# Both projections of a hybrid mLSTM and SSD layer as one level of seven-product block multiplication

## The chip, the cores and the metric

One NeuronCore of a Trainium2 chip runs the whole layer in one launch. The metric is device time in microseconds. PE is TensorE, PEld its weight loads, DVE VectorE, ACT ScalarE, POOL GpSimd; SP is SyncE, which issues nearly all transfers.

## The reference

The layer takes 2048 tokens of 1024 channels in float32:

```python
h = rms_norm(x, norm_w)
proj = h @ w_in                                  # 1024 x 6680
q, k, v, i_pre, f_pre, o_pre, z_m, z_s, xbc, dt_raw = jnp.split(proj, SPLIT_POINTS, axis=-1)
hm = mlstm_chunkwise(q, k, v, log_i, log_f)      # 4 heads, chunks of 128 tokens
hm = head_norm(hm) * mlstm_norm_w * sigmoid(o_pre) * silu(z_m)
xs, Bm, Cm = split(silu(causal_depthwise_conv(xbc, conv_w, conv_b)))
y = ssd_chunked(xs, dt, A, Bm, Cm) + d_skip * xs # 16 heads in 2 groups, chunks of 128 tokens
y = group_norm(y * silu(z_s)) * ssd_norm_w
x = x + concat([hm, y]) @ w_out                  # 2048 x 1024
return rms_norm(x, final_norm_w)
```

## The kernel before

The 2048 tokens are taken in four segments of 512. `prep_seg` normalises a segment and transposes it, so that channels lie on partitions. Every operand of a projection is held as two tiles, a rounded part (`hi`, an ACT copy, L140, L210, L711) and the rest (`lo`, a DVE subtraction, L141, L212, L712), and a product is three matmuls: hi by hi, hi by lo, lo by hi. `load_block` loads and splits a block of `w_in` columns, again for every segment. `ch_group` (L222 to L224) gives channels on partitions for 512 tokens, `tk_group` (L234 to L236) tokens on partitions for 128 tokens and 256 to 512 columns.

A segment runs through six phases (`PHASES`): four heads and two SSD groups. The recurrence of a phase (`rec_head`, `rec_group`) is woven in small steps into the projections of the next phase. Projected tiles stay in SBUF until it has read them. `rec_head` multiplies in split form too (L494 to L504, nine matmuls of 258 columns per chunk and head); `rec_group` uses plain float32 (L606, L617, L634). Its decay tile E is loaded as a broadcast of 128x1024 (L563), subtracted on POOL (L564), clipped on DVE, exponentiated on ACT (L566) and multiplied on DVE (L594); it has two buffers, and `decay(c + 1)` is issued between `states(c)` and `outs(c)`.

The mixed rows go to memory. The output projection (`load_out`, `load_mix`, `out_half`, L720 to L722) takes 16 blocks of 128 tokens by two halves of 512 columns and finishes with the residual add and the last norm.

The order of PE is the program's order. The other engines' queues are ordered by the framework's scheduler, which takes what is ready and, of that, what stands earlier in the program. Each `tag` of a pool is a ring of `bufs` tiles, and a new tile waits until one has been released.

Of the kernel before, what the change touches and what calls it, by code (L numbers as in the profile page):

```python
# [9 lines left out]
F32R = mybir.dt.float32r  # L10
AF = mybir.ActivationFunctionType
# [8 lines left out]
SEG = 512  # L20
NSEG = SEQ // SEG
NCH = SEG // P
NBLK = SEQ // P
MH = 4
# [25 lines left out]
def hybrid_layer(ctx, tc, x, norm_w, w_in, b_igate, b_fgate, conv_w, conv_b, dt_bias,  # L50
# [33 lines left out]
    rg = cst.tile([P, NBLK, SG], F32, name="rg")  # L84
# [15 lines left out]
    def load_consts():  # L100
# [9 lines left out]
        nc.vector.tensor_scalar_mul(nwo[:, 0:8], nwo[:, 0:8], float(DV) ** 0.5)  # L110

    mixd = [[dram.tile([P, 2, SEG], F32, name=f"mixh{s}_{h}") for h in range(MH)]
            + [dram.tile([P, 4, SEG], F32, name=f"mixg{s}_{g}") for g in range(SG)]
            for s in range(NSEG)]
    mrowd = [dram.tile([2, MH, SEG], F32, name=f"mrow{s}") for s in range(NSEG)]
    arowd = [dram.tile([NCH, SH, P], F32, name=f"arow{s}") for s in range(NSEG)]

    yd = [dram.tile([P, 512], F32, name=f"yd{b}") for b in range(NEARLY)]

    w8p = ctx.enter_context(tc.tile_pool(name="w8p", bufs=12))  # L120
    rawp = ctx.enter_context(tc.tile_pool(name="rawp", bufs=3))

    def w8_tile(nm):
        return w8p.tile([P, 4, 512], F32R, tag="w8", name=nm)

    def load_block(cols, lo_eng=None):
        n = sum(c[1] for c in cols)
        hi, lo = [], []
        for hf in range(2):
            th, tl = w8_tile("whi"), w8_tile("wlo")  # L130
            for q in range(2):
                k0 = hf * 4 + q * 2
                raw = rawp.tile([P, 2, 512], F32, tag="raw", name="raw")
                o = 0
                for (c0, w) in cols:
                    nc.sync.dma_start(
                        raw[:, :, o:o + w],
                        w_in[k0 * P:(k0 + 2) * P, c0:c0 + w].rearrange("(k p) c -> p k c", p=P))
                    o += w
                nc.scalar.copy(th[:, 2 * q:2 * q + 2, :n], raw[:, :, :n])  # L140
                (lo_eng or nc.vector).tensor_sub(tl[:, 2 * q:2 * q + 2, :n], raw[:, :, :n],  # L141
                                                 th[:, 2 * q:2 * q + 2, :n].bitcast(F32))
            hi += [th[:, i, :] for i in range(4)]
            lo += [tl[:, i, :] for i in range(4)]
        return hi, lo

    work = ExitStack()
    pp = work.enter_context(tc.tile_pool(name="pp", bufs=1))

    def pt(shape, tag, bufs, nm=None, dt=F32):  # L150
        return pp.tile(shape, dt, tag=tag, name=nm or tag, bufs=bufs)
# [14 lines left out]


    def load_chunk(s, c):
        r0 = s * SEG + c * P
        xt = pt([P, DM], "p4", 7, "xt") if s == 0 else rawp.tile([P, DM], F32, tag="raw", name="xt")  # L170
        nc.sync.dma_start(xt, x[r0:r0 + P, :])
        S["x", s, c] = xt

    def norm_chunk(s, c):
        if ("x", s, c) not in S:
            load_chunk(s, c)
        xt = S["x", s, c]
        ss = pt([P, 2], "ss", 3)
        for i in range(2):
            jk = pt([P, 512], "jk", 1, dt=mybir.dt.bfloat16)  # L180
            nc.scalar.activation(jk, xt[:, i * 512:(i + 1) * 512], AF.Square, accum_out=ss[:, i:i + 1])
        rs = pt([P, 1], "rs", 3)
        nc.vector.tensor_add(ss[:, 0:1], ss[:, 0:1], ss[:, 1:2])
        nc.gpsimd.tensor_scalar(rs, ss[:, 0:1], 1.0 / DM, EPS, op0=ALU.mult, op1=ALU.add)
        nc.gpsimd.tensor_tensor(rs, rs, mhalf, op=ALU.pow)
        nc.vector.tensor_scalar_mul(xt, xt, rs)
        S["n", s, c] = True

    def prep_seg(s):
        hi = [w8_tile("hhi") for _ in range(2)]  # L190
        lo = [w8_tile("hlo") for _ in range(2)]
        S[s, "hi"] = [hi[k // 4][:, k % 4, :] for k in range(KT)]
        S[s, "lo"] = [lo[k // 4][:, k % 4, :] for k in range(KT)]
        if s > 0:
            for c in range(NCH - 1):
                norm_chunk(s, c)
                yield
        for c in range(NCH):
            if ("n", s, c) not in S:
                norm_chunk(s, c)  # L200
            xt = S.pop(("x", s, c))
            for hf in range(2):
                ps = pj_tile()
                for i in range(4):
                    k = hf * 4 + i
                    nc.tensor.transpose(ps[:, i * P:(i + 1) * P], xt[:, k * P:(k + 1) * P], ident)
                d = slice(c * P, (c + 1) * P)
                for i in range(4):
                    k = hf * 4 + i
                    nc.scalar.activation(hi[hf][:, i, d], ps[:, i * P:(i + 1) * P], AF.Copy,  # L210
                                         scale=nwc[:, k:k + 1])
                    nc.vector.scalar_tensor_tensor(lo[hf][:, i, d], ps[:, i * P:(i + 1) * P],  # L212
                                                   nwc[:, k:k + 1], hi[hf][:, i, d].bitcast(F32),
                                                   op0=ALU.mult, op1=ALU.subtract)
            yield

    def ch_group(s, ps, W, col):
        hh, hl = S[s, "hi"], S[s, "lo"]
        whi, wlo = W
        c = slice(col, col + P)  # L220
        for k in range(KT):
# [3 lines left out]
            if k == KT // 2 - 1:  # L225
                yield

    def tk_group(s, ps, c, W, col, n):
# [4 lines left out]
        for k in range(KT):  # L233
# [3 lines left out]
            if k == KT // 2 - 1 and n == 512:  # L237
                yield
# [549 lines left out]
    def mesh(a, n, b, at):  # L788
# [4 lines left out]
        for _ in b:  # L793
            pass
# [99 lines left out]
```

## Time and profile before

| | |
|---|---|
| median of 3 runs | 1820.32 us (1819.45 to 1823.35) |
| profiled execution, first to last instruction | 1820.9 us; no other time of it is recorded |
| PE busy | 1771.4 us, 9508 matmul instructions |
| DVE, ACT, POOL busy | 1172.2, 869.5, 468.0 us |
| memory traffic | 220.51 MB, mean 121 GB/s |

Busy time is the union of an engine's instructions. A matmul's recorded end is modelled and lies behind the start of the next one, so the rate of PE is read from the distance between starts.

### The profile page before, as it was taken

The page shows a single profiled execution, that of the slowest core. Times are in us where ns is not written, and L with a number is a line of the kernel's source. Part 1 is how long each engine was busy: PE and PEld are TensorE (multiplying, and loading weights), DVE is VectorE, ACT ScalarE, POOL GpSimd, SP SyncE. Part 2 cuts the span into 40 slices and gives each one's busy share as a digit, 9 for nine tenths or more (in the row PEclk, how much of TensorE's full clock was granted, in tenths as well). Part 3 has the DMA queues.
Part 4 walks back from the last instruction along what each step waited for, and adds up shares of the span by engine and source line. Part 5 has one row for each costly group of instructions (what it writes and reads, how often), then busy time and mean ns, then how long its engine had stood idle before and what let it go on. Part 6 is the DMA issues. An engine that isn't in the chain of part 4 may idle for free.

```text
span 1820.9 us, 26575 instructions
## 1 busy us (share of the span) xinstructions
PE 1771.4 (97%) x9508; PEld 1493.1 (82%) x9508; DVE 1172.2 (64%) x2279; ACT 869.5 (48%) x1560; POOL 468.0 (26%) x602
## 2 busy tenths in 40 slices
PE   4999999999999999999999999999999989999998
PEld 3888888888888888888888888888888877888886
DVE  4647575777576648875766589757765886534442
ACT  4565445556555446564545465645455525212211
POOL 2114241413242413231334133313332240000000
PEclk9999999999999999999999999999999999999999
DMA  5434353256334432553354234524433458622220
GB/s 137 135 103 128 107 155 92 72 146 181 87 110 118 128 92 77 158 163 93 105 150 119 77 91 140 172 77 145 132 101 98 149 164 249 185 93 93 93 93 35
DMA packets 246692, 220.51 MB, mean 121 GB/s; under 512 B 25088, under 2 KB 207616, under 8 KB 246560
## 3 DMA queue, kind: packets, MB, share of 16 engines
q1 hardware_dynamic: 246528, 218.81, 40.5%
q8 instruction: 75, 1.23, 0.3%
q14 instruction: 57, 0.47, 0.1%
q0 software_dynamic: 32, 0.00, 0.0%
HBM read 192.09 MB, written 26.67 MB: 120 GB/s over the span
## 4 chain that ended last, share of the span: by engine, by line
PE 80%; DVE 6%; DMA 5%; issue 3%; ACT 3%; POOL 1%; SPq 1%; POOLq 0%; DVEq 0%; ACTq 0%
PE pj L222 11%; PE pj L223 10%; PE pj L224 10%; PE pj L234 7%; PE pj L236 7%; PE pj L235 7%; PE pj L722 6%; PE pj L721 6%; PE pj L720 6%; DMA raw<-in_w_in 1%; DVE wlo L141 1%; PE rc L634 1%; PE rc L617 1%; PE rc L606 1%; DMA ea<-arow 1%
## 5 line engine op out<-in xcount | busy, mean ns | idle before, releaser
L234 PE MATMUL pj<-whi,hhi 128*128 128x512 f32 (+2 forms) x1024 | 364.9, 356 | 11.0 <-ACT whi L140 9.7
L222 PE MATMUL pj<-hhi,whi 128*128 128x512 f32 x896 | 361.0, 403 | 2.0 <-DVE hlo L212 2.0
L235 PE MATMUL pj<-wlo,hhi 128*128 128x512 f32 (+2 forms) x1024 | 348.3, 340 | 3.5 <-POOL wlo L141 3.0
L236 PE MATMUL pj<-whi,hlo 128*128 128x512 f32 (+2 forms) x1024 | 349.1, 341 | 1.6 <-DVE hlo L212 1.6
L224 PE MATMUL pj<-hhi,wlo 128*128 128x512 f32 x896 | 350.0, 391 | 0.0
L223 PE MATMUL pj<-hlo,whi 128*128 128x512 f32 x896 | 349.8, 390 | 0.0
L141 DVE TENSOR_TENSOR wlo<-raw,whi 128x1024 fp32r<-128x1024 f32 (+2 forms) x236 | 276.1, 1183 | 57.8 <-ACT whi L140 57.2
L140 ACT CAST whi<-raw 128x1024 fp32r<-128x1024 f32 (+2 forms) x240 | 219.8, 935 | 141.6 <-DMA raw<-in_w_in 79.1
L234 PEld LDWEIGHTS pj<-whi,hhi 128*128 128x128 f32 x1024 | 195.5, 191 | 38.1 <-ACT whi L140 10.1
L235 PEld LDWEIGHTS pj<-wlo,hhi 128*128 128x128 f32 x1024 | 195.7, 191 | 28.1 <-issue 5.0
L236 PEld LDWEIGHTS pj<-whi,hlo 128*128 128x128 f32 x1024 | 195.3, 191 | 24.4 <-DVE hlo L212 2.5
L720 PE MATMUL pj<-wohi,mh 128*128 128x512 f32 x512 | 201.2, 393 | 0.3 <-ACT mh L711 0.3
L722 PE MATMUL pj<-wohi,ml 128*128 128x512 f32 x512 | 199.7, 390 | 1.0 <-DVE ml L712 1.0
L721 PE MATMUL pj<-wolo,mh 128*128 128x512 f32 x512 | 199.3, 389 | 0.0
L224 PEld LDWEIGHTS pj<-hhi,wlo 128*128 128x128 f32 x896 | 168.2, 188 | 36.5
L222 PEld LDWEIGHTS pj<-hhi,whi 128*128 128x128 f32 x896 | 168.4, 188 | 36.0 <-DVE hlo L212 2.7
L223 PEld LDWEIGHTS pj<-hlo,whi 128*128 128x128 f32 x896 | 168.7, 188 | 33.2 <-issue 1.7
L376 POOL TENSOR_TENSOR gt<-gt,sg 128x256 f32<-128x256 f32 x64 | 54.3, 848 | 256.6 <-DVE gt L375 231.1
L722 PEld LDWEIGHTS pj<-wohi,ml 128*128 128x128 f32 x512 | 96.1, 188 | 22.3 <-DVE ml L712 2.3
L720 PEld LDWEIGHTS pj<-wohi,mh 128*128 128x128 f32 x512 | 96.1, 188 | 21.0 <-ACT mh L711 0.7
L721 PEld LDWEIGHTS pj<-wolo,mh 128*128 128x128 f32 x512 | 96.2, 188 | 20.1 <-issue 0.5
L522 POOL TENSOR_SCALAR sq<-dn,sq 128x1 f32<-128x1 f32 x64 | 34.9, 546 | 277.5 <-ACT jk L521 88.1
(216 smaller groups left out, 2799.0 us busy)
## 6 DMA issues: line engine op xcount, KB each, us to landing
raw<-in_w_in SPq DMA_DIRECT2D x176, 256.0 KB, 3.4
raw<-in_w_in SPq DMA_DIRECT2D x64, 512.0 KB, 4.5
raw<-in_w_in SPq DMA_DIRECT2D x192, 128.0 KB, 2.4
E<-arow SPq DMA_DIRECT2D x32, 512.0 KB, 5.0
mt<-mixh SPq DMA_DIRECT2D x84, 128.0 KB, 3.3
mt<-mixg SPq DMA_DIRECT2D x42, 256.0 KB, 3.4
xt<-in_x SPq DMA_DIRECT2D x16, 512.0 KB, 3.4
ea<-arow SPq DMA_DIRECT2D x64, 128.0 KB, 3.0
```

The lines of the kernel that those rows point to most:

```text
L140: nc.scalar.copy(th[:, 2 * q:2 * q + 2, :n], raw[:, :, :n])
L141: (lo_eng or nc.vector).tensor_sub(tl[:, 2 * q:2 * q + 2, :n], raw[:, :, :n], th[:, 2 * q:2 * q + 2, :n].bitcast(F32))
L222: nc.tensor.matmul(ps, lhsT=whi[k][:, c], rhs=hh[k], start=(k == 0), stop=False)
L223: nc.tensor.matmul(ps, lhsT=whi[k][:, c], rhs=hl[k], start=False, stop=False)
L224: nc.tensor.matmul(ps, lhsT=wlo[k][:, c], rhs=hh[k], start=False, stop=(k == KT - 1))
L234: nc.tensor.matmul(ps, lhsT=hh[k][:, t], rhs=whi[k][:, w], start=(k == 0), stop=False)
L235: nc.tensor.matmul(ps, lhsT=hh[k][:, t], rhs=wlo[k][:, w], start=False, stop=False)
L236: nc.tensor.matmul(ps, lhsT=hl[k][:, t], rhs=whi[k][:, w], start=False, stop=(k == KT - 1))
L376: nc.gpsimd.tensor_mul(gt[:, c, :], gt[:, c, :], sg[:, 0:DV])
L720: nc.tensor.matmul(ps, lhsT=mh[:, k, :], rhs=wh, start=(k == k0), stop=False)
L721: nc.tensor.matmul(ps, lhsT=mh[:, k, :], rhs=wl, start=False, stop=False)
L722: nc.tensor.matmul(ps, lhsT=ml[:, k, :], rhs=wh, start=False, stop=(k == k1 - 1))
```

## The change

Both projections are computed with one level of a 7-product scheme: the matrices are cut in 2 x 2 blocks, and seven products of sums of blocks stand for eight products of blocks. The token axis is now cut in two halves of 1024 (`SUP`), each in two blocks of 512. Left operands are pairs of 128 columns of `w_in` (26 pairs per half), right operands the normalised, transposed tokens in seven combinations, held as 14 split tiles. For the output the left operands are pairs of 128-token blocks of the mixed rows, the right ones seven combinations of `w_out`, for each half of K; the first half's result goes to memory and is read back for the second.

`left_first` makes the left sums; in the second token half `left_w` reads them back from memory (`sumd`). `pair` evacuates and applies what follows a projection: gates as tanh in place of sigmoid (with the factors of 0.5 folded into constants), convolution steps 1024 wide, then a store to memory (`hd`, `gd`). `rec_head` and `rec_group` load per 128 tokens what they need, transpose the values in addition, and `rec_head` uses plain float32 matmuls. The group norm's factor is spread over the row by a product with ones (`spread`). The weave follows slots of products: 10 recurrence steps per head and 25 per group, over 28 slots (a head phase, four pairs) or 35 (a group phase, five pairs). Pools: `w4` 7 tiles of 1024 columns for nearly all staging, `big` 14, `e4` 1 in place of 2, 4 + 4 PSUM banks in place of 3 + 5. Core of the diff (`put` splits a tile with an ACT copy and a DVE subtraction, as `split` does):

```diff
+    def w4(nm, n=1024):
+        return mk([P, n], "w4", 7, nm)
...
+    def big(nm):
+        return mk([P, 4, TB], "big", 14, nm, F32R)
...
+    def split(nm, src, n, ops, names):
+        hi, lo = split_tiles(nm, n)
+        nc.scalar.copy(hi, src)
+        nc.vector.tensor_sub(lo, src, hi.bitcast(F32))
+        for i, o in enumerate(names):
+            ops[o] = tuple(t[:, i * 512:(i + 1) * 512].rearrange("p (k c) -> p k c", k=4)
+                           for t in (hi, lo))
+
+    def left_first(a, b):
+        ops = {}
+        s = w4("ls")
+        nc.vector.tensor_add(s[:, 0:512], b[:, 0:512], b[:, 512:])
+        split("la", a, 1024, ops, ["L11", "L12"])
+        nc.vector.tensor_sub(s[:, 512:], s[:, 0:512], a[:, 0:512])
+        split("lb", s, 1024, ops, ["S1", "S2"])
+        split("lc", b[:, 512:], 512, ops, ["L22"])
+        nc.vector.tensor_sub(b[:, 0:512], a[:, 0:512], b[:, 0:512])
+        nc.vector.tensor_sub(b[:, 512:], a[:, 512:], s[:, 512:])
+        split("ld", b, 1024, ops, ["S3", "S4"])
...
+    def product(ps, L, R, start):
+        lh, ll = L
+        rh, rl = R
+        for k in range(4):
+            for n, (l, r) in enumerate(((lh, rh), (lh, rl), (ll, rh))):
+                nc.tensor.matmul(ps, lhsT=l[:, k, :], rhs=r[:, k, :], start=start and k + n == 0,
+                                 stop=k == 3 and n == 2, skip_group_check=True)
+
+    def strassen(L, R, oa, ob, copy):
+        us = (oa[0], ob[0], ob[1])
+        pa = pj_tile()
+        product(pa, L["L11"], R["R11"], True)
+        nc.scalar.copy(us[0], pa)
+        yield 0
+        ps = pj_tile()
+        product(ps, L["L12"], R["R21"], True)
+        nc.vector.tensor_add(oa[0], ps, us[0])
+        yield 1
+        product(pa, L["S2"], R["T2"], False)
+        nc.scalar.copy(us[1], pa)
+        yield 2
+        pd = pj_tile()
+        product(pd, L["S3"], R["T3"], True)
+        yield 3
+        product(pa, L["S1"], R["T1"], False)
+        nc.scalar.copy(us[2], pa)
+        nc.vector.tensor_add(ob[1], pd, us[2])
+        yield 4
+        product(pa, L["S4"], R["R22"], False)
+        copy(oa[1], pa)
+        yield 5
+        product(pd, L["L22"], R["T4"], False)
+        nc.vector.tensor_add(ob[0], pd, us[1])
+        yield 6
...
+                for q in range(1, 4):
+                    nc.vector.scalar_tensor_tensor(dst, raw[:, q:q + SUP], cw[:, t, q:q + 1], dst,
+                                                   op0=ALU.mult, op1=ALU.add)
+                nc.scalar.activation(raw[:, 0:SUP], dst, AF.Tanh)
+                nc.vector.scalar_tensor_tensor(dst, raw[:, 0:SUP], 1.0, dst, op0=ALU.add, op1=ALU.mult)
+                nc.sync.dma_start(gd[s][n][:, j + i, :], dst)
...
+            d = slice(c * P, (c + 1) * P)
...
+                nc.sync.dma_start(t, x[r0:r0 + P, :])
...
+                nc.scalar.activation(jk, t, AF.Square, accum_out=ss)
+                nc.gpsimd.tensor_scalar(ss, ss, 1.0 / DM, EPS, op0=ALU.mult, op1=ALU.add)
+                nc.gpsimd.tensor_tensor(ss, ss, mhalf, op=ALU.pow)
+                nc.vector.scalar_tensor_tensor(t, t, ss, nwb, op0=ALU.mult, op1=ALU.mult)
...
+                    ps = q[kh, i] = pj_tile()
+                    for k in range(4):
+                        nc.tensor.transpose(ps[:, k * P:(k + 1) * P],
+                                            xt[i][:, (kh * 4 + k) * P:(kh * 4 + k + 1) * P], ident)
...
+            t12, t1, t2 = r2("t12"), r2("t1"), r2("t2")
+            put("R11", q[0, 0])
+            nc.scalar.copy(t12, q[0, 1])
+            nc.vector.tensor_sub(t1, t12, q[0, 0])
+            nc.vector.tensor_sub(t2, q[1, 1], t1)
+            put("T2", t2)
+            put("R21", q[1, 0])
+            put("T1", t1)
+            nc.vector.tensor_sub(t12, q[1, 1], t12)
+            put("T3", t12)
+            put("R22", q[1, 1])
+            nc.vector.tensor_sub(t2, q[1, 0], t2)
+            put("T4", t2)
+            yield
...
-                nc.tensor.matmul(ps[:, 0:NV], lhsT=ah, rhs=vh[:, c, :], start=True, stop=False)
...
+            for i in range(1, 4):
+                nc.tensor.transpose(ps[:, i * P:(i + 1) * P], t[:, i, :], ident)
...
+            nps = rc_tile()
+            nc.tensor.matmul(nps[:, 0:NV], lhsT=st, rhs=vt, start=True, stop=C is None)
+            if C is not None:
+                nc.tensor.matmul(nps[:, 0:NV], lhsT=qp, rhs=C, start=False, stop=True)
+            cps = rc_tile()
+            nc.tensor.matmul(cps[:, 0:NV], lhsT=kw, rhs=vt, start=True, stop=True)
...
-            E = pt([P, HPG, P], "e4", 2, "E")
...
+            E = mk([P, HPG, P], "e4", 1, "E")
+            nc.sync.dma_start(E, arowd[b][c, hs, :].partition_broadcast(P))
+            nc.gpsimd.tensor_tensor(E, bc(G["cum"][:, c, ws], P), E, op=ALU.subtract)
+            nc.scalar.activation(E, E, AF.Relu)
+            nc.scalar.activation(E, E, AF.Exp, scale=-1.0)
...
+            nc.tensor.matmul(ps[:, 0:P], lhsT=ones, rhs=dg, start=True, stop=True)
+            nc.vector.tensor_tensor(y, ps[:, 0:P].unsqueeze(1).broadcast_to([P, 4, P]), y, op=ALU.mult)
...
+            states(n)
+            yield
+            outs(n)
+            later(3, lambda n=n: norm(n))
+            later(5, lambda n=n: spread(n))
+            if n + 1 < len(seq):
+                decay(n + 1)
+                yield
+                tokens(n + 1)
+                if n + 2 < len(seq):
+                    load(n + 2)
+            yield
...
+        for _ in right_h(s):
+            if wv.prev is not None:
+                wv.to(wv.done + 1, wv.n)
+        drain(gates_mm(s))
...
+    def right_w(j):
...
+                    nc.sync.dma_start(w.rearrange("p (k c) -> p k c", k=2),
+                                      w_out[k0 * P:(k0 + 2) * P, b * TB:(b + 1) * TB]
+                                      .rearrange("(k p) c -> p k c", p=P))
+                    for k in range(2):
+                        nc.scalar.activation(w[:, k * TB:(k + 1) * TB], w[:, k * TB:(k + 1) * TB], AF.Copy,
+                                             scale=nwo[:, k0 + k:k0 + k + 1])
+
...
+            put("R11", t[0, 0])
+            t1 = w4("wt1")
+            nc.vector.tensor_sub(t1, t[0, 1], t[0, 0])
+            t2 = t[0, 0]
+            nc.vector.tensor_sub(t2, t[1, 1], t1)
...
+    for j in range(2):
+        for _ in right_w(j):
+            if wv.prev is not None:
+                for _ in range(4):
+                    wv.to(wv.done + 1, wv.n)
...
+        L = left_mix(j, 0)
+        for c in range(0, NBLK, 2):
+            a, b = w4("oa"), w4("ob")
+            for i, _ in enumerate(strassen(L, S["R", j + 10], halves(a), halves(b), evac_copy)):
+                if i == 1 and c + 2 < NBLK:
+                    nxt = left_mix(j, c + 2)
+                if wv.prev is not None:
+                    wv.to(wv.done + 1, wv.n)
...
+                xt = w4("xr")
+                nc.sync.dma_start(xt, x[ct * P:(ct + 1) * P, :] if j == 0 else ymd[ct])
```

## Rows read from the trace of the kernel before

**Rows 1.** The page, engines over the whole span: busy us (share), instructions.
```profile
PE 1771.4 (97%) x9508; PEld 1493.1 (82%) x9508; DVE 1172.2 (64%) x2279; ACT 869.5 (48%) x1560; POOL 468.0 (26%) x602
```

**Rows 2.** The page, chain of work that ended last, by engine.
```profile
PE 80%; DVE 6%; DMA 5%; issue 3%; ACT 3%; POOL 1%; SPq 1%; POOLq 0%; DVEq 0%; ACTq 0%
```

**Rows 3.** Groups by line and shape, PE: xcount | busy us, mean ns | idle before.
```profile
L222 PE MATMUL pj<-hhi,whi 128*128 128x512 f32 x896 | 361.0, 403 | 2.0 <-DVE hlo L212 2.0
...
L234 PE MATMUL pj<-whi,hhi 128*128 128x512 f32 x512 | 211.0, 412 | 0.0
...
L720 PE MATMUL pj<-wohi,mh 128*128 128x512 f32 x512 | 201.2, 393 | 0.3 <-ACT mh L711 0.3
...
L234 PE MATMUL pj<-whi,hhi 128*128 128x256 f32 x384 | 112.8, 294 | 0.0
...
L234 PE MATMUL pj<-whi,hhi 128*128 128x280 f32 x128 | 41.2, 322 | 11.0 <-ACT whi L140 9.7 <-ACT hhi L210 0.8 <-DVE graw L362 0.5
```

**Rows 4.** Timeline of PE, 300 to 308 us: start us, us, line, operation.
```profile
300.09 0.39 PE L222 MATMUL pj<-hhi,whi 128*128 128x512 f32 x1
...
302.81 0.39 PE L222 MATMUL pj<-hhi,whi 128*128 128x512 f32 x1
...
306.80 0.28 PE L502 MATMUL rc<-Ch,qh 128*128 128x258 f32 x1
...
307.52 0.39 PE L222 MATMUL pj<-hhi,whi 128*128 128x512 f32 x1
```

**Rows 5.** Timeline of PE, 403 to 406 us.
```profile
404.08 1.02 PE L617 MATMUL rc<-xw,bt 128*128 128x512 f32 x2
404.54 0.79 PE L234 MATMUL pj<-whi,hhi 128*128 128x512 f32 x1
405.17 0.39 PE L235 MATMUL pj<-wlo,hhi 128*128 128x512 f32 x1
```

**Rows 6.** Groups by line and shape, DVE and ACT.
```profile
L141 DVE TENSOR_TENSOR wlo<-raw,whi 128x1024 fp32r<-128x1024 f32 x176 | 235.7, 1349 | 25.4 <-ACT whi L140 24.9
...
L712 DVE TENSOR_TENSOR ml<-mt,mh 128x1024 fp32r<-128x1024 f32 x42 | 52.2, 1250 | 7.2 <-ACT mh L711 6.8 <-issue 0.2
...
L418 DVE SCALAR_TENSOR_TENSOR xs<-cv,cw,xs 128x512 f32<-128x512 f32 x96 | 71.5, 745 | 1.7
...
L711 ACT CAST mh<-mt 128x1024 fp32r<-128x1024 f32 x42 | 43.1, 1050 | 125.7 <-PE pj L721 85.8 <-DMA mt<-mixh 26.3 <-DMA mt<-mixg 13.5
...
L413 ACT COPY cv<-pj 128x512 f32<-128x512 f32 x48 | 27.9, 582 | 41.7 <-PE pj L224 41.7
...
L862 DVE TENSOR_TENSOR yo<-fx,fwbc 128x512 f32<-128x512 f32 x32 | 22.1, 691 | 5.9 <-DMA out<-yo 5.0
```

**Rows 7.** Timeline of PE, 0 to 23 us; in brackets idle and what ended it.
```profile
8.13 1.97 PE L206 MATMUL pj<-ident,xt 128*128 128x128 f32 x8 [8.13 <-DVE xt L186]
...
19.78 0.60 PE L234 MATMUL pj<-whi,hhi 128*128 128x280 f32 x1 [9.67 <-ACT whi L140]
...
22.09 0.43 PE L235 MATMUL pj<-wlo,hhi 128*128 128x280 f32 x1
...
22.32 0.43 PE L236 MATMUL pj<-whi,hlo 128*128 128x280 f32 x1
```

**Rows 8.** Windows: us, busy of each engine, granted clock, DMA share, GB/s.
```profile
20.00:45.00 25.00, 19.32 (x88) 15.79 (x89) 15.32 (x34) 15.71 (x37) 7.60 (x13) 0.86 0.58 130
420.00:480.00 60.00, 58.01 (x345) 49.63 (x344) 40.04 (x82) 35.62 (x56) 20.21 (x24) 1.00 0.52 146
```

**Rows 9.** Chain that ended last, 1806 to 1821 us: start us, us, what.
```profile
1813.93 0.76 DVE fx L728
```

**Rows 10.** Chain that ended last, 396 to 408 us.
```profile
397.00 6.00 DMA E<-arow
...
403.13 2.29 POOL E L564
```

**Rows 11.** The page, DMA queue: packets, MB, share of 16 engines.
```profile
q1 hardware_dynamic: 246528, 218.81, 40.5%
```

More of the change, by code (lines that the diff above doesn't have):

```diff
@@ L19 @@
 SEQ = 2048
-SEG = 512
-NSEG = SEQ // SEG
-NCH = SEG // P
+TB = 512
+NTB = SEQ // TB
+NCH = TB // P
 NBLK = SEQ // P
+SUP = 2 * TB
+NSUP = SEQ // SUP
 MH = 4
@@ L118, in hybrid_layer @@
[L118 to L151, printed above, removed]
+        nc.vector.tensor_scalar_mul(cw, cw, 0.5)
+        nc.vector.tensor_scalar_mul(cb, cb, 0.5)
+        nc.vector.tensor_scalar_mul(nwo[:, 0:8], nwo[:, 0:8], 0.25 * float(DV) ** 0.5)
+        nc.vector.tensor_scalar_mul(nwo[:, 8:16], nwo[:, 8:16], 0.5)
+    hd = [[dram.tile([P, 6, SUP], F32, name=f"hd{s}_{h}") for h in range(MH)] for s in range(NSUP)]
@@ L165, in tick @@
                 fn()
[L168 to L187, printed above, removed]
@@ L542, in rec_head @@
+        load(0)
         yield
-        split_state()
         scores(0)
+        load(1)
         yield
-        for c in range(NCH):
-            memory(c)
-            later(3, lambda c=c: turn(c))
-            if c + 1 < NCH:
-                scores(c + 1)
+        for n in range(len(seq)):
+            memory(n)
+            later(4, lambda n=n: turn(n))
+            if n + 1 < len(seq):
+                scores(n + 1)
+            if n + 2 < len(seq):
+                load(n + 2)
             yield
@@ L553, in rec_group @@
     def rec_group(s, g):
-        xs, zg, bT, cT = S.pop((s, "s", g))
-        G = S[s, "g"]
+        seq = [(2 * s + i, c) for i in range(2) for c in range(NCH)]
         hs = slice(g * HPG, (g + 1) * HPG)
@@ L816, in hybrid_layer @@
-    next(prev)
-    tick(2)
-    for q in range(1, 4):
-        load_out(0, q, w8_tile, raw_tile)
-    for i, _ in enumerate(chain(*(early(b, work_x) for b in range(3)))):
-        if i % 4 != 0:
-            next(prev, None)
-        tick()
-    for _ in prev:
-        tick(2)
-    tick(9)
-    work.close()
-    fin = ctx.enter_context(tc.tile_pool(name="fin", bufs=1))
-    def fw8_tile(nm):
-        return fin.tile([P, 4, 512], F32R, tag="fw8", name=nm, bufs=8)
-    def fraw_tile():
-        return fin.tile([P, 2, 512], F32, tag="fraw", name="fraw", bufs=2)
@@ new lines, in hybrid_layer, with drain, __init__, set @@
+    NREC = {"h": 10, "g": 25}
+    def drain(g):
+        for _ in g:
+            pass
+    class Weave:
+        def __init__(self):
+            self.prev, self.n, self.done = None, 0, 0
+        def set(self, g, n):
+            self.finish()
+            self.prev, self.n, self.done = g, n, 0
+        def to(self, i, total):
+            tick()
+            while self.prev is not None and self.done < self.n and self.done * total < i * self.n:
+                next(self.prev, None)
+                self.done += 1
+        def finish(self):
+            if self.prev is not None:
+                drain(self.prev)
+            self.prev = None
@@ new lines, in hybrid_layer @@
+    wv = Weave()
+    load_consts()
+    flat = [(s, ph, pc) for s in range(NSUP) for ph in PHASES for pc in pair_cols(ph)]
+    nextL = []
+    idx = 0
+    for s in range(NSUP):
+        for _ in right_h(s):
+            if wv.prev is not None:
+                wv.to(wv.done + 1, wv.n)
+        drain(gates_mm(s))
+        nextL.append(left_w(s, *pair_cols(PHASES[0])[0][2:]))
+        gq = [gates(2 * s), gates(2 * s + 1)]
+        for ph in PHASES:
+            pcs = pair_cols(ph)
+            slot, total = 0, 7 * len(pcs)
+            for pc in pcs:
+                kind, j, ca, cb_ = pc
+                L = nextL.pop()
+                for i, _ in enumerate(pair(s, ph, kind, j, ca, cb_, L)):
+                    if i == 1:
+                        idx += 1
+                        if idx < len(flat) and flat[idx][0] == s:
+                            s2, _, pc2 = flat[idx]
+                            nextL.append(left_w(s2, pc2[2], pc2[3]))
+                    if gq and slot % 2 == 1:
+                        if next(gq[0], "end") == "end":
+                            gq.pop(0)
+                    slot += 1
+                    wv.to(slot, total)
+            for g in gq:
+                drain(g)
+            gq = []
+            wv.set(rec(s, ph), NREC[ph[0]])
```

864 lines of the change are left out of this document (367 added, 497 removed).

## Prediction

> **What bounds the kernel now.** I read the page's engine line first: TensorE (PE) is busy 1771.4 of 1820.9 us, VectorE (DVE) 1172.2, ScalarE (ACT) 869.5 [rows 1]. The chain that ended last lies 80% on PE [rows 2], so a change pays by what it takes from PE and costs by every microsecond in which PE waits. Next the matmul groups by shape [rows 3]: three groups each of 896, 512 and 512 with 512 columns (5760), three of 384 with 256 columns (1152), three of 128 with 280 (384). Their means of 0.39 us are no prices, since matmuls overlap; the price is the distance between starts. Twelve 512-column matmuls start in 302.81 - 300.09 = 2.72 us, 0.227 each; the six 258-column ones between 306.80 and 307.52 take 0.12 each [rows 4]. The projections are then 5760 x 0.227 + 1152 x 0.12 + 384 x 0.13 = 1496 us of PE, and 1771 - 1496 = 275 us are recurrences, transposes and gates. The median of the runs (1820.3) and the profiled span (1820.9) are one number; all sums are made on the span.
>
> **What leaves PE.** A pair of column blocks is 7 products of 12 matmuls, 84 in all. 26 pairs x 2 token halves and 16 output pairs (two K halves of eight) make 68 pairs, 5712 matmuls of 512 columns, and the gates 96 more: 5808 x 0.227 = 1318 us. So the count of 512-column matmuls does not fall; what goes is the 1536 narrow ones. Saving: 178 us. One product is 2.72 us, a pair 19.1.
>
> **What the recurrences add to PE.** `memory` trades nine split matmuls (9 x 0.12 = 1.08 us) for three in plain float32 with 258 columns. The float32 price [rows 5]: L617 starts at 404.08 as two instructions, the next matmul (L234) is stamped 404.54 but takes 0.79 us where its kind takes 0.39, and the one behind it starts at 405.17. From 404.08 to 405.17 is 1.09, less 0.227 for L234: 0.86 us for 512 columns, 0.43 for 258. Three are 1.30: +0.22 x 64 chunk-heads = 14 us. The value tile is now transposed per chunk, 2 x 64 transposes between 0.06 (128 columns at the projections' rate) and 0.21 (at the float32 rate); at 0.11, 14 us. `spread` adds one float32 product of 128 columns, 32 x 0.21 = 7. PE after: 1771 - 178 + 35 = 1628 us. Without new waits, and with the old 49.5 us of PE idle, the change would give 1678. The rest of the sum is where PE will wait.
>
> **1. Operand sets, four places.** The right-hand operands (14 `big` tiles, exactly one set) are rebuilt at the start, between the token halves, and before each K half of the output. DVE sets the pace. A two-input DVE operation costs 1.25 to 1.35 us at 1024 columns and 0.69 at 512 [rows 6]. `right_h` has per chunk two of 1024 and eleven of 512: 2.6 + 7.6 = 10.2 us, four chunks 41 us. ACT with 7 us per chunk is behind it.
> Start: PE transposed first at 8.13 us and multiplied from 19.78 [rows 7]; now two tiles and a broadcast are needed before the first transposes, say 12 us; 12 + 41 - 2.6 (the first scaling lies inside the 12) = 50, less 64 transposes x 0.11 = 7: idle 43 (38 to 48).
> Between the halves: 41, plus 10 for the last pair's tail and the group recurrence, less 5 for chunks scaled early = 46, less 10 us that PE has to do: 36 (26 to 46). The transposes stand behind the last product in PE's queue, so little can start early.
> `right_w`: per half of K rows, 11 operations of 1024 columns, 14.3 us, so 28.6 for a set. Each tile comes free behind its own product of the last pair, so about 9 us can be done under that pair. For the first K half the eight recurrence steps give PE 8 us in about 30: idle 22 (15 to 32). For the second, PE has nothing else, and the pool `w4` (7 tiles, 5 wanted per half, up to 4 still held by the last pair) delays the loads: 24 (14 to 32). The sum is 125 us.
>
> **2. Clock and end.** After 9.67 us idle the 280-column matmuls start 0.233 us apart (22.09 to 22.32), as far as 512 columns elsewhere [rows 7]: half rate, 1.2 of 2.4 GHz, with a mean granted clock of 0.86 over 20 to 45 us [rows 8]. A mean of 0.86 over 25 us is 7 us at half rate, 3.5 us lost, so four pauses can lose 14: take 8 (0 to 14). The end was 7 us behind the last matmul [rows 9]; a full-width add, square, scale and store make it 9.
>
> **3. The wait before the sixth product.** In `strassen` the sixth product adds onto `pa`, which ACT must first copy out behind the fifth. No product stands between. The fifth's last matmul ends 0.39 - 0.227 = 0.16 us after the next could have started; the copy is 0.58 [rows 6], two hand-offs about 0.1: 0.85 us. The next pair's `lb` split (1024 columns, 1.05 us) becomes free at that same instant and stands earlier in the program; if ACT takes it first the wait is 1.9. A recurrence step that falls just there covers it, in about a third of the 68 pairs (10 head steps in 28 or 35 slots, 25 group steps in 28). 45 waits x 0.85 to 1.9 = 38 to 86: take 62. Behind PE's wait stands everything PE has in order, so nothing else fills it.
>
> **4. Group recurrence and DVE inside the pairs.** `e4` falls from two buffers to one, and the decay tile is loaded only behind `outs`. The loop is then load 6.0, POOL 2.3 [rows 10], two ACT passes of 1.05, DVE 1.3 [rows 6]: 11.7, with queues about 14 us. PE has 3.4 slots x 2.72 + 4 us of recurrence = 13.5 us between two `outs`: 0.5 to 1.5 us late, 32 times, about 25. DVE per convolution pair of the first half: five sums or subtractions of 512 and three of 1024 on the left operands 7.4, three PSUM adds 2.1, eight convolution steps of 2 x 0.745 = 11.9, the head recurrence 4: 25 us against 23.3 of PE; six such pairs are 10 us, and hand-offs as much again: 20. Together 45 (10 to 100).
>
> **What costs nothing.** Traffic grows from 219 MB to about 316 MB (projections written and read 54 MB each, the sums of weights 27 each way), with some 200,000 packets of 512 B. At the present cost per packet, 0.405 x 16 x 1821 us / 246,528 = 0.048 us [rows 11], some 310,000 packets keep the engines half busy: hidden by the pair's 20 us, in which a load has about 10 us of slack. If that cover goes (`w4` full), loads are late by their landing time; that sits in the upper end of part 4. Sigmoids become tanh, and more copies come to ACT, which has 869.5 us now [rows 1] and is off the path except in part 3.
>
> **Sum.** Idle 125 + 8 + 9 + 62 + 45 = 249; 1628 + 249 = 1877 us, 3% slower. All lower ends give 1778, all upper ends 1995.
>
> **Rivals.** (a) The operand sets overlap with their neighbours. For: every `big` tile is free behind its own product. Against: one set only, transposes behind the last product, `w4` of seven. If three quarters of the 125 us vanish: 1783. It decides from half, 60 us, on, and then the change is faster. 0.27. (b) DVE becomes the bound. It has 1172 us now [rows 1]; left operands 430, PSUM adds 143, convolution steps 143, other gates 67, recurrences 390 (2.5 us per chunk-head, 7.2 per chunk-group), operand sets 139, last stage 40 make 1352, and beside group and convolution work it is 90% full and more. With part 4 and part 3 at their upper ends, 1877 + 55 + 24 = 1956. 0.12. (c) Float32 costs what the start stamps say, 0.46 for 512 columns [rows 5]: 258 columns 0.23, three 0.70, and parts change by 38 + 3: 1836. Against: the 0.79 us of L234. 0.07. (d) The clock falls in every pair. The waits of part 3 come every 20 us; at 3.5 us for each of 68, 1877 + 238 = 2115. 0.03: from 420 to 480 us PE stood still for 2 us in all and the clock stayed at 1.00 [rows 8].
> The Trainium skill speaks for (d): "TensorE: Matmul & The Clock Gate", section "A second HAM failure mode: psum-queue depth-cycling", says that brief idling between matmul groups can make the clock swing between its two levels. By that rule the time is that of (d); by the row on the start, only long pauses do it. The trace does not show it for short ones.
>
> **Chances and range.** Forecast (1830 to 1945) 0.51; (a) 0.27, of which 0.03 within 0.2% of before; (b) 0.12; (c) 0.07, of which 0.02 within 0.2%; (d) 0.03. A 0.2% difference (3.6 us) is about what a measurement of this kernel can tell from none. Faster 0.24, same 0.05, slower 0.51 + 0.12 + 0.05 + 0.03 = 0.71. The range 1790 to 1945 leaves out the best of (a) (0.10), the worst of (b) (0.06) and (d).
>
> **What would show it.** In the changed profile: 12 matmuls of 512 columns still start in 2.72 us; PE stands still 30 us and more at four places, with DVE full in them; before the sixth product PE waits 0.9 to 1.9 us for ACT's copy; `outs` waits for DVE's product on E; DVE is busy over 1350 us. The prediction is wrong if PE flows through the operand sets, if float32 is cheap, or if PE waits over 5 us in ordinary pairs.

## The result and the profile after

The changed kernel takes 2133.81 us (median of 4 runs, 2123.6 to 2139.02), the kernel before beside it 1819.88 (1818.55 to 1823.35): a ratio of 1.171 [1.168, 1.175]. It is 17% slower, where 3% were forecast; the time lies 189 us above the upper end of the range.

The page of the changed kernel: engines, the chain that ended last by engine, the busiest DMA queue.

```profile
PE 1762.4 (82%) x8040; PEld 1386.3 (65%) x8040; DVE 1242.2 (58%) x1913; ACT 905.0 (42%) x1676; POOL 335.8 (16%) x509
...
PE 28%; DMA 9%; DVE 7%; ACT 6%; POOL 4%; issue 3%; SPq 0%; POOLq 0%; ACTq 0%; DVEq 0%
...
q1 hardware_dynamic: 301264, 314.04, 48.0%
```

Against [rows 1, 2, 11]: DVE and ACT are busy for about as long as before and neither is full, the transfers take half of the DMA engines' time, as forecast, and PE is busy 9 us less in a span that is 316 us longer. The page's busy time hides two things: PE stands still for 374 us, and 168 us of its busy time pass at the lower clock. Windows of the changed kernel (the third number from the right is the granted clock):

```profile
0.00:100.00 100.00, 52.00 (x218) 35.94 (x219) 59.05 (x112) 39.12 (x68) 11.89 (x23) 0.85 0.31 86
100.00:800.00 700.00, 616.72 (x2785) 491.29 (x2784) 415.34 (x685) 294.37 (x576) 82.27 (x166) 0.96 0.52 156
800.00:900.00 100.00, 55.32 (x242) 38.76 (x241) 57.72 (x98) 44.13 (x79) 15.07 (x22) 0.74 0.36 117
900.00:1640.00 740.00, 657.12 (x3098) 524.02 (x3098) 414.73 (x678) 328.79 (x647) 110.81 (x201) 0.95 0.52 153
1640.00:1700.00 60.00, 24.07 (x131) 18.70 (x130) 43.91 (x48) 36.82 (x57) 9.49 (x7) 0.71 0.50 154
...
1930.00:1960.00 30.00, 12.67 (x45) 9.67 (x46) 26.44 (x28) 17.27 (x21) 0.00 (x0) 0.64 0.43 140
```

Four stretches (0 to 100, 800 to 900, 1640 to 1700, 1930 to 1960) are the operand sets: PE busy 40 to 55% of the time and the clock lowest. But the ordinary pairs in the two long stretches between them (100 to 800, 900 to 1640) also lose 11 to 12% to idle time, at a clock of 0.95 to 0.96. What PE waits for, all waits of a pair of lines together (total us, times, longest):

```profile
PE pj L230 <- ACT ob L250: 85.9, 49, 5.9
PE pj L333 <- DVE xt L326: 47.0, 4, 26.4
PE rc L650 <- ACT bt L619: 40.5, 7, 29.1
PE pj L230 <- ACT lah L179: 26.1, 1, 26.1
PE pj L230 <- ACT cbt L250: 23.1, 12, 4.2
PE rc L428 <- DVE cs L423: 21.3, 4, 8.8
PE rc L527 <- ACT vt L517: 19.8, 7, 3.9
PE rc L650 <- DVE xw L623: 15.3, 8, 6.5
...
PE rc L668 <- DVE E L626: 5.8, 3, 4.2
```

The first and the fifth row are the sixth product waiting for the copy behind the fifth (`us[2]`, L250): 109 us in 61 waits, the largest cost. One of them on PE and on ACT:

```profile
408.28 0.50 PE L230 MATMUL pj<-R22h,ldh 128*128 128x512 f32 x1 [4.11 <-ACT ob L250]
...
409.16 0.63 PE L230 MATMUL pj<-R22h,ldh 128*128 128x512 f32 x1
409.58 0.63 PE L230 MATMUL pj<-R22l,ldh 128*128 128x512 f32 x1
```

```profile
404.29 1.06 ACT L596 ACTIVATE E<-E 128x1024 f32<-128x1024 f32 x1 [3.28 <-POOL E L595]
405.25 1.03 ACT L179 CAST lbh<-ls 128x1024 fp32r<-128x1024 f32 x1
406.19 1.05 ACT L597 ACTIVATE E<-E 128x1024 f32<-128x1024 f32 x1
407.14 0.61 ACT L602 ACTIVATE ea<-ea 128x512 f32<-128x512 f32 x1
407.66 0.56 ACT L250 COPY ob<-pj 128x512 f32<-128x512 f32 x1
```

The copy of 0.56 us comes after a split of the next pair and three passes of the group recurrence. Of the 61 waits 54 have that split ahead of the copy, and up to six operations stand there. Behind the wait of 4.11 us PE starts matmuls 0.42 to 0.43 us apart (409.16, 409.58): its lower level, 1.2 GHz. And even at the full clock they are not 0.227 apart as in [rows 4] but 0.235 (twelve of them from 559.88 to 562.70):

```profile
559.88 0.39 PE L230 MATMUL pj<-R11h,lah 128*128 128x512 f32 x1
...
562.70 0.40 PE L230 MATMUL pj<-R21h,lah 128*128 128x512 f32 x1
```

**The account.** By the trace, PE's gaps are 361.7 us and the tail behind the last matmul 11.8. Half rate was granted for 297.8 us in 39 stretches (before: 9.5 us in two), 168 of it while PE was busy: 84 us lost. Some 5700 matmuls start 0.006 us later each than in the kernel before (0.234 against 0.228 over all that follow on directly): 33 us. The rest of PE's work is 2136.9 - 361.7 - 11.8 - 84 - 33 = 1646 us; 1628 was forecast. The profiled span lies 260 us over the forecast: idle 130 (362 against 125 + 62 + 45), clock 76, spacing 33, work 18, end 3.

### The profile page after: what moved, and what is told of

It reads as the page before. It is cut to its first block, busy times and chain, and to the rows that moved or that the text cites. A ratio compares the mean times of both kernels' runs of the same rounds, so it can differ in the third digit from the quotient of the medians.

```text
span 2136.9 us, 23408 instructions
## 1 busy us (share of the span) xinstructions
PE 1762.4 (82%) x8040; PEld 1386.3 (65%) x8040; DVE 1242.2 (58%) x1913; ACT 905.0 (42%) x1676; POOL 335.8 (16%) x509
## 4 chain that ended last, share of the span: by engine, by line
PE 28%; DMA 9%; DVE 7%; ACT 6%; POOL 4%; issue 3%; SPq 0%; POOLq 0%; ACTq 0%; DVEq 0%
PE pj L230 23%; DMA E<-arow 2%; DMA nmi<-mrow 2%; POOL E L595 2%; DMA wo<-in_w_out 1%; DVE cd L280 1%; ACT lbh L179 1%; DMA mix<-g 1%; POOL oa L855 1%; PE rc L668 1%; DMA ea<-arow 1%; PE rc L650 1%; DVE mx L194 1%; ACT ob L250 1%; ACT E L597 1%
## 5 line engine op out<-in xcount | busy, mean ns | idle before, releaser
L230 PE MATMUL pj<-R22h,ldh 128*128 128x512 f32 x272 | 125.2, 460 | 109.3 <-ACT ob L250 85.9
L230 PEld LDWEIGHTS pj<-R22h,ldh 128*128 128x128 f32 x272 | 56.1, 206 | 142.5 <-ACT ob L250 105.0
L230 PE MATMUL pj<-R11h,lah 128*128 128x512 f32 x272 | 111.0, 408 | 26.1 <-ACT lah L179 26.1
L230 PE MATMUL pj<-T1h,lbh 128*128 128x512 f32 x272 | 117.1, 431 | 10.5 <-ACT cbt L244 7.2
L230 PE MATMUL pj<-T2h,lbh 128*128 128x512 f32 x272 | 119.6, 440 | 6.5 <-ACT oa L237 5.2
L230 PE MATMUL pj<-R22l,ldh 128*128 128x512 f32 x272 | 116.8, 429 | 0.0
L230 PE MATMUL pj<-R22h,ldl 128*128 128x512 f32 x272 | 116.5, 428 | 0.0
L230 PE MATMUL pj<-T4h,lch 128*128 128x512 f32 x272 | 114.6, 421 | 0.0
L230 PE MATMUL pj<-R11h,lal 128*128 128x512 f32 x272 | 108.7, 400 | 6.0 <-DVE lal L180 6.0
L230 PE MATMUL pj<-T3h,ldh 128*128 128x512 f32 x272 | 112.7, 414 | 0.0
L230 PE MATMUL pj<-R21h,lah 128*128 128x512 f32 x272 | 112.3, 413 | 0.0
L230 PE MATMUL pj<-T1l,lbh 128*128 128x512 f32 x272 | 111.9, 412 | 0.0
L230 PE MATMUL pj<-T1h,lbl 128*128 128x512 f32 x272 | 110.7, 407 | 0.0
L230 PE MATMUL pj<-T2h,lbl 128*128 128x512 f32 x272 | 110.4, 406 | 0.0
L230 PE MATMUL pj<-T2l,lbh 128*128 128x512 f32 x272 | 110.4, 406 | 0.0
L230 PE MATMUL pj<-T3l,ldh 128*128 128x512 f32 x272 | 108.5, 399 | 0.0
L230 PE MATMUL pj<-R11l,lah 128*128 128x512 f32 x272 | 108.5, 399 | 0.0
L230 PE MATMUL pj<-T3h,ldl 128*128 128x512 f32 x272 | 108.5, 399 | 0.0
L230 PE MATMUL pj<-R21l,lah 128*128 128x512 f32 x272 | 108.1, 397 | 0.0
L230 PE MATMUL pj<-R21h,lal 128*128 128x512 f32 x272 | 107.9, 397 | 0.0
```

What stands on the lines that cost most here:

```text
L230: nc.tensor.matmul(ps, lhsT=l[:, k, :], rhs=r[:, k, :], start=start and k + n == 0, stop=k == 3 and n == 2, skip_group_check=True)
```

## The experiments

The kernel before, on the chips of these runs, took 1824 to 1825 us; ratios are against it.

**Addresses.** The changed kernel's tiles lie differently in SBUF: the `big` tiles start at 128 modulo 256 bytes, where the operands of before lay at multiples of 1024. The split tiles of the left operands start at 224 modulo 256. This kernel moves addresses alone: both kinds of operand tiles to multiples of 1024, and the rotating staging tiles with them.

```diff
+    pad = cst.tile([P, 224], F32, name="pad")
...
-            a, b = w4("ca", SUP + 3), w4("cbt", SUP + 3)
+            a, b = w4("ca", SUP + 32), w4("cbt", SUP + 32)
```

> Only addresses change: operand tiles start at multiples of 1024 bytes, as in the kernel before. Theory address: undisturbed 512-column matmuls start 0.228 us apart again in place of 0.234, and the time falls by 5712 x 0.006 = 34 us to about 2100. Theory traffic (the spacing comes from other engines and transfers): 0.234 stays, and so does the time, within 10 us of 2134.

2117.23 us (2116.0 to 2119.58), ratio 1.161 [1.159, 1.163]. Twelve matmuls take 2.72 us again, as in [rows 4]:

```profile
561.01 0.39 PE L232 MATMUL pj<-T3h,ldl 128*128 128x512 f32 x1
...
563.73 0.39 PE L232 MATMUL pj<-T1h,lbl 128*128 128x512 f32 x1
```

So the spacing came from the addresses. Which of the moved operands does it was not separated. Of the 33 us, 17 came by the medians, 21 in the profiled runs: PE's busy time fell by 29 us and its gaps grew from 362 to 369. That PE now reaches the next late copy sooner would explain the growth; it is not shown apart from the spread of the runs.

**A bank of its own for the sixth product,** so that it no longer waits for the third copy; VectorE adds the parts afterwards.

```diff
-        us = (oa[0], ob[0], ob[1])
+        us = (oa[0], ob[0], oa[1])
...
-        product(pa, L["S4"], R["R22"], False)
-        copy(oa[1], pa)
+        pe = pj_tile()
+        product(pe, L["S4"], R["R22"], True)
+        nc.vector.tensor_add(oa[1], pe, us[2])
+        if copy is not evac_copy:
+            copy(oa[1], oa[1])
```

> The sixth product gets a PSUM bank of its own and DVE adds it, so nothing stands between the fifth and the sixth product. Theory wait and clock: the 109 us of waits before the sixth product go, and with them half of the 88 us that PE loses at the half clock: 2134 - 109 - 44 = about 1980, mean granted clock 0.95 or more. Theory shift (ACT and DVE are late anyway): the wait moves to the seventh product or the next pair, the time stays above 2090. Theory wait alone: minus 109 us and the clock stays at 0.93, about 2025.

2050.24 us (2038.68 to 2050.67), ratio 1.123 [1.119, 1.126]: 84 us back, between the theory of the wait alone and that of the shift. The rows L230 on L250 are gone; in their place the recurrence's waits grew (`bt` from 40.5 us, `vt` from 19.8):

```profile
PE rc L653 <- ACT bt L622: 47.8, 10, 28.9
...
PE rc L530 <- ACT vt L520: 31.3, 10, 3.7
```

Gaps are 285 us (-76), the loss to half clock 61 (-23). The profiled run is the fastest of the four, so these two add up to more than 84. ScalarE is also relieved of 52 copies of 0.58 us, those of the sixth product, which VectorE's sum replaces; what that alone is worth was not separated.

**The three copies put ahead in ScalarE's order,** bank and dependences as in the change.

```diff
-        nc.scalar.copy(us[2], pa)
+        with tc.high_priority():
+            nc.scalar.copy(us[2], pa)
```

(and so for the first two)

> The three copies out of the shared PSUM bank are put ahead of whatever else is ready on ACT. Theory queue: the mean wait before the sixth product, now 109 us over 61 waits = 1.8 us, falls to about 0.9, since the split of the next operands no longer goes first: minus 55 us, and minus some 30 to 40 of clock: about 2040. Theory copy: the wait is the copy itself and the hand-offs, 2110 or more.

2127.3 us (2122.28 to 2129.17), ratio 1.166 [1.163, 1.169]. The wait before the sixth product is still 88 us in 60 waits, this row and 16.9 us in 12 for `cbt`:

```profile
PE pj L230 <- ACT ob L253: 71.2, 48, 5.0
```

Priority mends little here; taking the dependence away mended it. The edit hardly changed the order it was meant to change: in 50 of the 60 waits the next pair's split still stands ahead of the copy (54 of 61 in the change). So the run does not show what a copy that goes first would be worth.

**Two operand sets left out.** The sets of the second token half and of the second K half are not built, the first ones are used again; this leaves out that part of the computation.

```diff
-        for _ in right_h(s):
+        if s == 1:
+            S["R", 1] = S["R", 0]
+        for _ in (right_h(s) if s == 0 else range(NCH)):
```

(and so for `right_w`)

> The right-hand operand sets of the second token half and of the second half of K are not rebuilt; the first ones are used again (this leaves out part of the computation). Theory sets: the waits at 820 to 875 us (44 + 11) and at 1915 to 1950 us (32), 87 us, and the half clock around them (some 55 us at half rate, 15 us lost) go, as do 64 transposes (7 us): 2134 - 109 = about 2025. By the terms of the prediction alone (36 + 24 + 7 + 4): 2063. Theory hidden: the work after the places is late too, over 2090.

2040.16 us (2033.17 to 2042.32), ratio 1.118 [1.115, 1.121]: 94 us back. Gaps fell by 74 us to 288, the loss to half clock by 23 to 61. About a quarter of what these sets cost is the clock.

**The clock, in the kernel before.** At 27 places of its last stage, where PE otherwise never waits (1525 to 1800 us: granted clock 1.00), PE is made to wait for ScalarE, by one copy out of PSUM or by four in a chain:

```diff
+            if g == 1 and hold:
+                w = hold[0].tile([P, 512], F32, tag="hw", name="hw", bufs=1)
+                nc.scalar.copy(w, ps)
+                for _ in range(3):
+                    nc.scalar.copy(w, w)
+                nc.tensor.matmul(rc_tile()[:, 0:1], lhsT=w[:, 0:P], rhs=ones[:, 0:1], start=True, stop=True)
```

(`range(0)` in the first of the two)

> The kernel before, with 27 places added in its last stage at which TensorE waits for one small copy by ScalarE out of PSUM before it goes on (results unchanged). Theory (only waits from some 2 us on are followed by half clock): 27 waits of about 0.85 us, 23 us in all, and the granted clock of the last stage stays at 1.00: about 1845. Rival (any wait of TensorE for another engine brings half clock, as long as those of the changed kernel): 27 times 1.7 us more, about 1890, granted clock clearly under 1.00 there.

> The same 27 places, with four copies by ScalarE in a chain, so that each wait is 2.7 to 2.9 us. Theory (waits from some 2 us on are followed by half clock): the waits themselves 73 us, and up to 27 times 1.7 us lost to half clock behind them, 46 us: about 1940, with the granted clock of the last stage under 1.00 and each stretch of half clock beginning behind one of the 27 waits. Rival (the half clock of the changed kernel has another cause than the waits): 73 us alone, about 1895, at granted clock 1.00.

With one copy 1904.51 us (1900.56 to 1907.74), ratio 1.044 [1.041, 1.047]; with four 2014.27 (2013.27 to 2019.6), ratio 1.105 [1.102, 1.107]. PE's waits and the windows of the last stage, of the first kernel and then of the second:

```profile
PE rc L735 <- ACT hw L732: 52.8, 27, 3.4
```

```profile
1535.00:1900.00 365.00, 310.97 (x1302) 248.77 (x1302) 121.84 (x185) 73.59 (x133) 8.76 (x16) 0.96 0.26 82
```

```profile
PE rc L735 <- ACT hw L734: 125.4, 27, 6.8
```

```profile
1535.00:2008.00 473.00, 352.86 (x1300) 280.01 (x1300) 120.46 (x183) 116.44 (x210) 8.76 (x16) 0.85 0.20 62
```

Both waits were longer than expected, 2.0 and 4.6 us on average, because the copy again stood behind others in ScalarE's queue (two casts L712 of about 1 us ahead of the one at 1758.11). For the same work PE is busy 311 us in the one and 353 in the other. Of the 27 waits of 1.5 to 3.4 us, 7 are followed by a stretch of half clock: none of the 13 of 1.46 us, 6 of the 13 of 2.34 and the one of 3.36. Of the 27 of 3.9 to 6.8 us, all are (by the trace's clock record). So the theory is borne out at these lengths, and its rival, that any wait does it, falls. PE after such a wait, at 0.43 us between matmuls:

```profile
1722.21 0.45 PE L735 MATMUL rc<-ones,hw 128*128 128x1 f32 x2 [4.77 <-ACT hw L734]
...
1725.23 0.63 PE L721 MATMUL pj<-wohi,mh 128*128 128x512 f32 x1
1725.66 0.47 PE L722 MATMUL pj<-wolo,mh 128*128 128x512 f32 x1
```

The sums nearly close: four copies, 125 us of waits and 70 lost to half clock (3 before) make 192, measured 190; one copy, 53 and 23 (3 before) make 73, measured 80. The small matmuls, the other waits and the tail lie in the rest. So a wait is enough to bring the lower clock, in a kernel without any of the change, and the longer it is the oftener. The figure of 1.7 us for each was too small: 67 / 27 = 2.5.

**Own bank and addresses together.**

> The changed kernel with the sixth product in a PSUM bank of its own and with the operand tiles moved to multiples of 256 bytes. Theory (the two causes are separate): own bank took 84 us off 2134 and the addresses make 0.234 us between matmuls of 512 columns 0.227, 0.006 to 0.007 us for each of some 5700, so 34 us more: about 2016. Rival (the faster matmuls only reach the next wait sooner, as when the addresses were moved alone and 17 of 34 us came): about 2033.

2036.95 us (2030.78 to 2047.51), ratio 1.117 [1.113, 1.121]: 13 us under the own bank alone. The rival holds: by the profiled runs gaps of 301 us (+16) and a loss to half clock of 77 (+16) took back nearly all of the 34 us, by the medians 21. The own bank's profiled run is its fastest, so the first figure is the upper one.

**The recurrence's copies.** First put ahead in ScalarE's order, then made by VectorE (both on the kernel with own bank and addresses):

```diff
-            nc.scalar.copy(bt, cps[:, P:2 * P])
+            nc.vector.tensor_copy(bt, cps[:, P:2 * P])
```

(so for `vt` and `kw`; in the first the ScalarE copy stands in `with tc.high_priority()`)

> As the kernel with own bank and moved addresses, and the three copies of ScalarE for which TensorE waits in the recurrence (bt, vt, kw) are put ahead of E's passes in ScalarE's order. Theory (TensorE waits there because the copies stand in ScalarE's in-order queue behind E's passes, which wait for VectorE): the waits for bt (some 48 us) and vt (some 31 us) fall by about 50 us together, and the half clock behind them with it: about 1970 to 1985. Rival (the chain from TensorE through ScalarE and back is itself that long): no change, within 10 us of that kernel.

> As the kernel with own bank and moved addresses (2037 us), but the three copies out of PSUM for which TensorE waits in the recurrence (bt, vt, kw) are made by VectorE instead of ScalarE. Theory (ScalarE's queue is in order and its head often waits for VectorE or GpSimd, so a copy that is ready stands behind it): the waits for bt (44.6 us, 30.2 of it at the operand set) and vt (38.1 us) fall by 30 to 40 us in sum, with half clock behind them some 10 more: about 1990 to 2000. Rival (VectorE, 64% busy and in order too, is as late): the same waits end with VectorE's copies, and the time stays within 10 us of 2037.

Put ahead: 2029.18 us (2027.46 to 2034.35), ratio 1.113 [1.110, 1.116], 8 us: the rival's no change within 10 us. There `bt` fell to 22.1 us, but `vt` stayed at 36.6 and `lah` rose to 42.1. By VectorE: 1999.93 (1996.72 to 2007.55), ratio 1.095 [1.093, 1.098], 37 us. Waits of the kernel that both start from, and of the one with VectorE's copies:

```profile
PE rc L655 <- ACT bt L624: 44.6, 9, 30.2
PE rc L532 <- ACT vt L522: 38.1, 10, 4.1
PE pj L232 <- ACT lah L181: 27.2, 1, 27.2
...
PE rc L655 <- DVE xw L628: 16.5, 5, 6.0
```

```profile
PE pj L232 <- ACT lah L181: 42.1, 2, 27.2
PE rc L655 <- DVE xw L628: 29.2, 12, 6.6
...
PE rc L532 <- DVE vt L522: 14.9, 7, 4.9
PE rc L655 <- DVE bt L624: 12.1, 3, 9.8
...
PE rc L532 <- POOL sq L551: 11.3, 6, 3.7
```

The waits for `bt` and `vt` fall by 56 us, and 39 us come up at what is late next (`xw`, POOL's `sq`, and `lah`, the end of the operand set that `bt` had covered). The theory of ScalarE's queue holds; the priority was the wrong lever. In the chunk behind 1066 us of the kernel with priority, the transposes that `vt` copies end at 1065.70, but `vt` (0.37 us) is made at 1076.85, behind a tanh of the conv pair that waited for VectorE and a scaling that waited for POOL's power:

```profile
1072.13 1.06 ACT L287 ACTIVATE cbt<-cd 128x1024 f32<-128x1024 f32 x1 [2.81 <-DVE dn L546]
...
1076.22 0.47 ACT L554 ACTIVATE mx<-rc,sq 128x256 f32<-128x256 f32 x1 [1.91 <-POOL sq L553]
...
1076.85 0.37 ACT L524 COPY vt<-rc 128x256 f32<-128x256 f32 x1
```

The Trainium skill, "Perfetto Trace Analysis", section "Tensor Engine Instruction (MATMUL, LD_WEIGHTS)", says that ScalarE, VectorE and GpSimd take their instructions strictly in order; these rows agree.

**Own bank, addresses, and two sets left out** (the edits of above; the same part of the computation is left out).

> The kernel with own bank and moved addresses, and the operand sets of the second token half and of the second K half are not rebuilt (the first ones are used again, which leaves out that part of the computation). Theory (the three causes are separate places and add up): 2037 less the 94 us that the two sets alone were worth, about 1943; what then still lies over the kernel before are the recurrence's waits, the first operand sets and the half clock behind them. Rival (the waits trade places): over 1965.

1959.28 us (1952.42 to 1966.04), ratio 1.073 [1.070, 1.077]: 78 us, of the 94 that the sets were worth alone. The causes nearly add up, and 135 us over the kernel before remain with all three gone: 231 us of gaps, 80 lost to half clock. Of the versions that compute the whole layer the best is the one with VectorE's copies, 10% behind the kernel before. No run reaches it.

## Why the prediction was wrong, step by step

**Right.** The direction, and the terms of PE's own work: 1646 us against 1628. The float32 price: from 305.86 to the second L230 at 307.40 lie 1.54 us, less 0.235 for the first L230, 1.31 for three products of 258 columns; 1.30 was forecast, so rival (c) falls.

```profile
305.86 0.60 PE L527 MATMUL rc<-vt,st 128*128 128x258 f32 x2
...
306.98 0.58 PE L230 MATMUL pj<-T1h,lbh 128*128 128x512 f32 x1
307.40 0.39 PE L230 MATMUL pj<-T1l,lbh 128*128 128x512 f32 x1
```

Traffic and packets came as forecast, and PE itself waits for a load only twice, 1.8 us in all. But they are not wholly hidden: the chain that ended last lies 9% on DMA (5% before [rows 2]), 2% each on the loads of E and `nmi`, for which other engines wait. What that costs was not separated. DVE is no bound: 1242 us, against 1352 in rival (b).

**Part 1, the sets: right in kind, 147 us against 125.** The start is 43.5 (43 forecast), the boundary of the token halves 42 (36), `right_w` 29 and 32 (22 and 24). They do not overlap with their neighbours, so rival (a) falls. That DVE sets the pace fits its busy share: 95% of the time from 26 to 61 us, 91% from 1663 to 1692 and 81% from 1915 to 1950. At the boundary (811 to 876) it is 72%; there 10.6 of the 42 us are a wait for the gates' weights (`wgh`), whose cast stands on ACT behind the group recurrence's passes over E. What the part lacked is that the first K half's set holds up the recurrence too: `bt`, a copy of 0.26 us, stands at 1691.70 behind 16 us of the set's work on ACT, and PE waits 29.1 us for it.

**Part 2, the clock: the step that failed by most, 84 us against 8.** It let only the four long pauses bring the lower clock, from one example of 9.67 us [rows 7] and, in rival (d), from a stretch with 2 us of idle time in 60 [rows 8]. Neither bears it out. The 0.86 of [rows 8] does not belong to the long pause, whose half-rate matmuls (22.09, 22.32) lie ahead of the clock record's first entry at 26.3 us. It comes from 33 to 40 us, behind waits of 2.12, 0.82 (at 31.36) and 0.72 us (windows of the kernel before, then its PE timeline):

```profile
20.00:33.00 13.00, 8.25 (x38) 6.74 (x38) 7.66 (x18) 9.61 (x24) 7.60 (x13) 1.00 0.71 146
33.00:40.00 7.00, 6.10 (x24) 5.31 (x24) 4.59 (x8) 3.20 (x6) 0.00 (x0) 0.51 0.69 177
```

```profile
27.91 0.40 PE L235 MATMUL pj<-wlo,hhi 128*128 128x280 f32 x1 [2.12 <-POOL wlo L141]
...
32.61 0.40 PE L236 MATMUL pj<-whi,hlo 128*128 128x280 f32 x1 [0.72 <-DVE hlo L212]
```

And the 2 us of the full stretch are mainly one wait:

```profile
471.54 0.39 PE L504 MATMUL rc<-Ch,ql 128*128 128x258 f32 x1 [1.66 <-DVE ql L476]
```

So the trace of before did show half clock behind short waits, and against it one wait of 1.66 us that passed; 45 waits of 0.85 to 1.9 us could not be put at nothing from it. In the changed kernel 34 of the 38 stretches of half clock ahead of the end have a wait of 2.1 us or more just ahead of or in them, the other four one of 1.6 to 1.9, and the two added-wait kernels show that the waits bring it about. Rival (d) had this mechanism. The Trainium skill, "TensorE: Matmul & The Clock Gate", section "A second HAM failure mode: psum-queue depth-cycling", tells of a kernel in which brief idling between matmul groups makes the clock swing between its two levels; this trace agrees, with a mean granted clock of 0.95 from 900 to 1640 us. But the 2115 of (d) is near the result by accident. It put 238 us on the clock, for every pair; the clock cost 84, in the 38 stretches, and waits beyond the forecast 130. The prediction's own sign of being wrong came too, waits of over 5 us in ordinary pairs: up to 5.9 before the sixth product, 6.5 for `xw`, 8.8 for `cs`.

**Part 3, the wait before the sixth product: right place, wrong size, 109 us against 62.** 61 waits of 1.8 us, where 45 of 0.85 to 1.9 were put. The part allowed one split ahead of the copy on ACT; in the rows at 404 to 408 us four operations stand there, three of them of the recurrence.

**Part 4: wrong in its waits, and over its range.** What is left of the gaps is 362 - 147 - 109 = 106 us, where 45 (10 to 100) were put. The loop over E, 25 us in the forecast, costs 5.8. In its place come waits of PE for single results of the woven steps that stand late in other engines' queues: `vt` 19.8, `xw` 15.3, `bt` 11.4 besides the one at the set, and the gates' chain `cs`, 21.3 in four waits, which the part did not have at all.

**Not foreseen: the tiles' addresses,** 33 us in PE's rate, of which 17 came back alone.

The sum of all upper ends, 1995 us, lies 142 under the profiled span: 70 of the clock (84 against 14), 33 of the spacing, 23 of part 3, 18 of PE's work, 6 of part 4 and 3 of the end, with part 1 11 under its own. That the parts are also coupled (a longer wait on ACT is a longer wait on everything behind it, and brings half clock) fits the experiments, in which a mended wait came back in part elsewhere; how much of the 142 us that makes was not separated.

What stays open: which moved operand sets the spacing, and what each wait behind the last 135 us is worth. Of the 231 us of gaps in the kernel with all three gone, 42 lie at the start, 26 at the first K half's set, and most of the rest in waits for `vt` (38), `bt` (20 besides the set), `cs` (21) and `xw` (19).

## What to carry to other kernels

Before you count the multiplications saved, write down what each removed gap on TensorE was covered by: the kernel before had products in three PSUM banks in turn and hardly ever waited, the scheme chains four products through one bank. Price a TensorE wait by what can stand ahead of its releaser in that engine's in-order queue, not by the releaser's own duration, and add the clock to each wait of some microseconds. Read a mean granted clock in short windows before you put it down to a pause, and a stretch's idle time by its single waits. To mend such a wait, take the dependence away or move the copy to a queue whose head does not block: a second bank gave 84 us and VectorE 37; reordering gave 6 to 8, no more than the spread of the runs.

## What the runs showed of the hardware

- The addresses of matmul operands in SBUF changed the distance between matmuls of 512 columns from 0.227 to 0.235 us, and moving them changed it back, with no other edit.
- In an otherwise full stage at clock 1.00, waits of 3.9 to 6.8 us brought the clock to its lower level every time, waits of 2.34 us in 6 of 13, waits of 1.46 us in none of 13. In the first case the half rate cost 2.5 us each, half as much again as the wait of 4.6 us itself.
